# A state space mixer whose gate takes two GpSimd operations, whose squares go to ScalarE, and whose norm sums share a PSUM bank with another group's spread

## The chip, the cores and the metric

The kernel runs on one core of a Trainium2 chip, as one program and one launch. The metric is device time in microseconds (us), the median of the runs of one kernel. The engines are named as the profile names them: PE is TensorE, with PEld its weight loads, DVE is VectorE, ACT is ScalarE, POOL is GpSimd (Pool below), and SP is the engine that issues most of the DMAs.

## The reference

The trunk has two layers over a sequence of 256 tokens with a model width of 1024: `x += 1/2 SwiGLU(norm x)`, `x += mixer(norm x)`, `x += 1/2 SwiGLU(norm x)`. The mixer of layer 0 is a Mamba-2 state space mixer, that of layer 1 is latent attention. Only the first is touched by the change. Cut to what matters:

```python
proj = h @ w_in                       # 1024 -> z (2048), x and B and C (4096), dt (32)
xbc = silu(conv(xbc, conv_w, conv_b)) # depthwise, 4 taps
dt = softplus(dt + dt_bias); a = -exp(a_log)
y = ssd_chunked(xs, dt, a, bm, cm) + d_skip * xs
g = (y * silu(z)).reshape(b, s, 8, 256)
g = g * rsqrt(mean(g * g, axis=-1) + EPS)   # one norm for each of 8 groups
x = x + (g.reshape(b, s, 2048) * norm_w) @ w_out
```

The 2048 channels form 8 groups of 256 channels (4 heads of 64). Each group has a B and a C of 128 states, and a norm of its own at the end.

## The kernel before

**Data.** Channels lie on the 128 partitions, so a group of 256 channels is two halves of 128, and tokens lie along the free axis (`T` is 256). Every weight is streamed from memory once. A unit is up to eight tiles of 128x128: SP issues its DMA (`raw`), ScalarE casts it to the fast float format (`whi`, L131), and VectorE subtracts to get what the cast lost (`wlo`, L134). A product is three matmuls, high by high, high by low and low by high (`mm3`, L227 to L229), or two wider ones (L238) in the feed-forward parts. So ScalarE and VectorE owe TensorE one `whi` and one `wlo` for each unit, and everything else that they do stands in the same queues.

**The mixer.** `ssm()` has stages, called for groups 0 to 7 in an interleaved order:

- `stage_bc`, `stage_x`, `stage_z` project with the input weights. VectorE scales the projection (`up`, L421, or `zt`, L683). For B, C and x a convolution follows: ScalarE makes the first two taps (`ca` and `cb`), Pool adds them (L436), VectorE adds the other two taps (L439) and ScalarE applies Silu (L443). For z, ScalarE applies Silu alone (`zs`, L685).
- `sums` makes running sums of the decay. VectorE copies them as `bias` (L530), ScalarE as `ac` (L536), and a DMA takes them to memory (`acd`). `stage_a` fetches them for its group (`acb`, a DMA), ScalarE takes the exponentials into `dec` (L569 and L572, eight a group), and VectorE multiplies them with a product of B and C (`cbm`), L576. `stage_a` runs for two groups at a time, so there are 16 exponentials together, with a table load ahead and one behind.
- `stage_t` transposes x (`xd`, L595). `stage_y` is the scan: eight matmuls (L609 and L612), `y` on VectorE (L619), and then on Pool the gate `gt = y * zs` (L624, 128x512), two squares of 128x256 (`add_square`, L263 and L266) and their sum `gsq` (L267).
- `stage_n` sums `gsq` over the partitions on TensorE (L273, a product with ones), VectorE makes mean plus EPS (`rsv`, L277), and Pool raises it to -1/2 (`rsc`, L281).
- `stage_o` spreads `rsc` over the partitions with two transposes (L288), VectorE forms the normed `gn` (L639), and ScalarE and VectorE cut it in `yh` (L252) and `yl` (L253). `stage_out` multiplies them with the output weights into four banks that stay open through all groups.

PSUM has two pools here, each of four banks: `acc`, and `misc`, from which each call of `misc_ps()` takes the next bank. `zt`, `y` and `gn` share three buffers (tag `tmp`).

**The order.** The program is written group by group as below; a scheduler then merges the stages, so instructions of several groups alternate on each engine. Each engine runs its own queue in order, and waits on semaphores. ScalarE's functions that need a table are kept in their written order (`in_turn`).

Of the kernel before, what the change touches and what calls it, by code (L numbers as in the profile page):

```python
# [185 lines left out]
def trunk(ctx: ExitStack, tc: tile.TileContext, xt, pos, wts, small, consts, out):  # L186
# [36 lines left out]
    def misc_ps():  # L223
        return psm.tile([P, 2 * T], F32, tag="misc", name="misc")
# [41 lines left out]
        nc.gpsimd.tensor_tensor(out=sq, in0=src, in1=src, op=ALU.mult)  # L266
        nc.gpsimd.tensor_tensor(out=acc, in0=acc, in1=sq, op=ALU.add)  # L267

    def rs_col(acc, n):

        ps = misc_ps()
        for b in range(NB):
            nc.tensor.matmul(  # L273
                ps[:, b : b + 1], acc[:, b * P : (b + 1) * P], ones, start=True, stop=True
            )
        v = sp.tile([P, NB], F32, tag="rsv", name="rsv")
        nc.vector.tensor_scalar(  # L277
            out=v, in0=ps[:, :NB], scalar1=1.0 / n, scalar2=EPS, op0=ALU.mult, op1=ALU.add
        )
        r = sp.tile([P, NB], F32, tag="rsc", name="rsc", bufs=4)  # L280
        nc.gpsimd.tensor_tensor(out=r, in0=v, in1=mhalf[:, :NB], op=ALU.pow)  # L281
        return r

    def spread(r):

        ps = misc_ps()
        for b in range(NB):
            nc.tensor.transpose(  # L288
                ps[:, b * P : (b + 1) * P], r[:, b : b + 1].broadcast_to([P, P]), ident
            )  # L290
        return ps
# [113 lines left out]
    def ssm(n, nxt):  # L405
        with tc.tile_pool(name="mp", bufs=2) as mp:
# [10 lines left out]
            def conv(ps, tiles, dst):  # L417

                up = ups[count[0] % 2]
                count[0] += 1  # L420
                nc.vector.tensor_tensor(  # L421
                    out=up[:, :, KC - 1 :], in0=wide(ps), in1=pair(rs), op=ALU.mult
                )
                a = mp.tile([P, 2, T], F32, tag="ca", name="ca")
                b = mp.tile([P, 2, T], F32, tag="cb", name="cb")

                def w(t, k):
                    return sm[:, S_CW + t * KC + k : S_CW + t * KC + k + 1]

                for j, t in enumerate(tiles):  # L430
                    nc.scalar.activation(
                        a[:, j], up[:, j, 0:T], AF.Identity,
                        bias=sm[:, S_CB + t : S_CB + t + 1], scale=w(t, 0),
                    )
                    nc.scalar.activation(b[:, j], up[:, j, 1 : 1 + T], AF.Copy, scale=w(t, 1))
                nc.gpsimd.tensor_tensor(out=a, in0=a, in1=b, op=ALU.add)  # L436
                for k in (2, 3):
                    for j, t in enumerate(tiles):
                        nc.vector.scalar_tensor_tensor(  # L439
                            out=a[:, j], in0=up[:, j, k : k + T], scalar=w(t, k), in1=a[:, j],  # L440
                            op0=ALU.mult, op1=ALU.add,
                        )
                in_turn(nc.scalar.activation(dst, a, AF.Silu))  # L443
# [159 lines left out]
            def stage_y(g):  # L603
# [17 lines left out]
                        in1=ps[:, j * T : (j + 1) * T], op0=ALU.mult, op1=ALU.add,  # L621
                    )
                gt = mp.tile([P, 2, T], F32, tag="gt", name="gt")
                nc.gpsimd.tensor_tensor(out=gt, in0=y, in1=zs, op=ALU.mult)  # L624
                sq = sp.tile([P, T], F32, tag="xsq", name="gsq")
                for j in range(2):
                    add_square(sq, gt[:, j], j == 0)
                st[g, "g"], st[g, "q"] = gt, sq

            def stage_n(g):  # L630
                st[g, "r"] = rs_col(st.pop((g, "q")), 2 * P)

            def stage_o(g):
                gt = st.pop((g, "g"))
                ps = spread(st.pop((g, "r")))
                gn = mp.tile([P, 2, T], F32, tag="tmp", name="gn", bufs=3)
                for j in range(2):
                    t = 2 * g + j
                    nc.vector.scalar_tensor_tensor(  # L639
                        out=gn[:, j], in0=gt[:, j], scalar=sm[:, S_SN + t : S_SN + t + 1],  # L640
                        in1=ps[:, :T], op0=ALU.mult, op1=ALU.mult,
                    )
                yh = mp.tile([P, 2, T], F32R, tag="yh", name="yh", bufs=3)
                yl = mp.tile([P, 2, T], F32R, tag="yl", name="yl", bufs=3)
                two_part(yh, yl, gn)
                st[g, "y"] = yh, yl
# [31 lines left out]
            def stage_z(g):  # L678
# [6 lines left out]
                in_turn(nc.scalar.activation(zs, zt, AF.Silu))  # L685
                st[g, "z"] = zs

            stage_bc(1)
            last = NG - 1
            for g in range(NG):  # L690
                stage_x(g)
                if g == 0:
                    bias, acd = sums()
                if g > 1:
                    stage_o(g - 2)
                stage_z(g)
                if g:
                    stage_y(g - 1)
                if g % 2 == 0:
                    stage_a(g)  # L700
                    stage_a(g + 1)
                if g + 2 < NG:
                    stage_bc(g + 2)
                if g:
                    stage_n(g - 1)
                if g < last:
                    stage_t(g)
                if g > 2:
                    stage_out(g - 3)
# [582 lines left out]
```

## Time and profile before

| | |
|---|---|
| median of three runs | 1103.98 us (1102.43 to 1105.25) |
| the profiled execution | 1104.49 us, of which the span from first to last instruction is 1102.7 us |
| TensorE busy | 1079.8 us, 98% of the span |
| VectorE, ScalarE, Pool busy | 838.8, 643.1 and 195.7 us |
| mean granted TensorE clock | 0.992 of full speed |

The mixer with its norm runs from about 205 to 440 us of the span. The 1.8 us between the profiled execution and its span are not in the trace. A granted clock of 1.00 is TensorE's upper level, 2.4 GHz; a stretch that shows less has spent a part of itself at the lower one, 1.2 GHz.

### The profile page before, as it was taken

To read this page: it belongs to the slowest core of one execution; us is meant where nothing else is said; L and a number is where in the kernel's file an instruction comes from. 1 tells how busy PE (TensorE), PEld (TensorE's weight loads), DVE (VectorE), ACT (ScalarE), POOL (GpSimd) and SP (SyncE) were. 2 spreads that over 40 slices of the span, in tenths; PEclk is the share of its full clock that TensorE was granted. 3 is DMA by queue.
4 is the path that set the end of the run, shared out by engine and by line. 5 is a ranking of instruction groups with operands and counts; after the bars stand their busy time and mean duration, and the time that the engine had idled before them with its cause. 6 is when DMAs were issued, how large, how long until landed. Compare 5 with 4: busy or idle time off the path is not lost.

```text
span 1102.7 us, 18308 instructions
## 1 busy us (share of the span) xinstructions
PE 1079.8 (98%) x6886; PEld 964.3 (87%) x6886; DVE 838.8 (76%) x1396; ACT 643.1 (58%) x1105; POOL 195.7 (18%) x201
## 2 busy tenths in 40 slices
PE   8999999999899998999999999999999999999998
PEld 7888888998899998888888988888898688888887
DVE  7877766789978867877777688876779868877663
ACT  6755644667876744666544476664458546655541
POOL 1100013213523235000012101001240544000000
PEclk9999999999999998999999999999999999999999
DMA  8656655565445453655555566655531325656661
GB/s 287 213 189 190 184 188 170 173 197 190 161 163 178 135 185 97 208 187 184 184 191 189 174 210 211 212 196 187 175 105 59 97 87 167 214 186 188 191 200 49
DMA packets 55640, 191.58 MB, mean 174 GB/s; under 512 B 6240, under 2 KB 9088, under 8 KB 55552
## 3 DMA queue, kind: packets, MB, share of 16 engines
q1 hardware_dynamic: 55488, 190.41, 53.0%
q8 instruction: 54, 0.88, 0.3%
q14 instruction: 34, 0.28, 0.1%
q0 software_dynamic: 64, 0.01, 0.0%
HBM read 189.31 MB, written 1.08 MB: 173 GB/s over the span
## 4 chain that ended last, share of the span: by engine, by line
PE 61%; DVE 2%; ACT 0%; issue 0%; ACTq 0%; DVEq 0%
PE acc L238 32%; PE misc L238 17%; PE acc L227 2%; PE acc L228 2%; PE acc L229 2%; PE acc L1072 1%; PE acc L248 1%; PE acc L247 1%; PE acc L249 1%; PE misc L963 1%; PE misc L1032 1%; PE misc L1057 0%; DVE pr L1050 0%; DVE mx L1041 0%; PE misc L1033 0%; PE misc L273 0%
## 5 line engine op out<-in xcount | busy, mean ns | idle before, releaser
L134 DVE TENSOR_TENSOR wlo<-raw,whi 128x1024 fp32r<-128x1024 f32 (+2 forms) x345 | 429.4, 1247 | 155.0 <-ACT whi L131 153.8
L131 ACT CAST whi<-raw 128x1024 fp32r<-128x1024 f32 (+2 forms) x353 | 362.8, 1032 | 252.5 <-PE acc L238 132.9
L238 PE MATMUL misc<-xp,whi 128*128 128x512 f32 x704 | 277.9, 398 | 0.5 <-DVE xp L257 0.5
L238 PE MATMUL acc<-xp,whi 128*128 128x512 f32 x704 | 275.5, 395 | 0.0
L238 PE MATMUL acc<-ap,whi 128*128 128x512 f32 x616 | 215.5, 397 | 0.0
L238 PE MATMUL acc<-xp,wlo 128*128 128x256 f32 x704 | 196.8, 281 | 0.0
L238 PE MATMUL misc<-xp,wlo 128*128 128x256 f32 x704 | 196.4, 281 | 0.3 <-DVE wlo L134 0.2
L238 PE MATMUL acc<-ap,wlo 128*128 128x256 f32 x616 | 167.8, 281 | 0.0
L238 PEld LDWEIGHTS acc<-xp,whi 128*128 128x128 f32 x704 | 131.9, 188 | 32.2
L238 PEld LDWEIGHTS misc<-xp,whi 128*128 128x128 f32 x704 | 131.9, 188 | 24.2 <-DVE xp L257 0.8
L238 PEld LDWEIGHTS misc<-xp,wlo 128*128 128x128 f32 x704 | 132.5, 188 | 8.2 <-DVE wlo L134 0.9
L238 PEld LDWEIGHTS acc<-ap,whi 128*128 128x128 f32 x616 | 113.9, 188 | 25.5
L238 PEld LDWEIGHTS acc<-xp,wlo 128*128 128x128 f32 x704 | 132.8, 189 | 0.7
L238 PEld LDWEIGHTS acc<-ap,wlo 128*128 128x128 f32 x616 | 115.4, 188 | 2.8
L346 ACT COPY g<-misc 128x256 f32<-128x256 f32 x88 | 32.7, 371 | 77.1 <-PE misc L238 77.1
L228 PE MATMUL acc<-xp,whi 128*128 128x256 f32 x264 | 74.6, 283 | 0.0
L227 PE MATMUL acc<-xp,whi 128*128 128x256 f32 x264 | 74.5, 283 | 0.0
L229 PE MATMUL acc<-xp,wlo 128*128 128x256 f32 x264 | 74.2, 281 | 0.0
L263 POOL TENSOR_TENSOR xsq<-x 128x256 f32<-128x256 f32 x5 | 3.1, 612 | 284.8 <-DVE x L402 271.4
L266 POOL TENSOR_TENSOR sq<-x 128x256 f32<-128x256 f32 x35 | 31.7, 912 | 111.2 <-DVE x L402 111.2
L347 DVE TENSOR_TENSOR g<-misc,g 128x256 f32<-128x256 f32 x88 | 37.0, 420 | 18.0 <-ACT g L346 18.0
L227 PEld LDWEIGHTS acc<-xp,whi 128*128 128x128 f32 x264 | 49.7, 189 | 0.3 <-issue 0.3
(260 smaller groups left out, 1889.5 us busy)
## 6 DMA issues: line engine op xcount, KB each, us to landing
raw<-wts SPq DMA_DIRECT2D x341, 512.0 KB, 3.7
acb<-acd SPq DMA_DIRECT2D x8, 512.0 KB, 3.8
raw<-wts SPq DMA_DIRECT2D x8, 256.0 KB, 4.9
raw<-wts SPq DMA_DIRECT2D x4, 384.0 KB, 3.2
x<-xt SPq DMA_DIRECT2D x8, 128.0 KB, 4.5
out<-x SPq DMA_DIRECT2D x8, 128.0 KB, 3.5
raw<-wts SPq DMA_DIRECT2D x4, 192.0 KB, 2.4
sm<-small SPq DMA_DIRECT2D x1, 283.5 KB, 6.4
```

The costliest lines, as they stand in the source:

```text
L131: self.nc.scalar.copy(hi[:, c], raw[:, c])
L134: ins = eng.tensor_tensor(out=lo[:, c], in0=raw[:, c], in1=hi[:, c].bitcast(F32), op=ALU.subtract)
L227: nc.tensor.matmul(o, w[0], h, start=start, stop=False)
L228: nc.tensor.matmul(o, w[0], l, start=False, stop=False)
L229: nc.tensor.matmul(o, w[1], h, start=False, stop=stop)
L238: nc.tensor.matmul(dst, a, b, start=start and i == 0, stop=stop and i == 1)
L247: nc.tensor.matmul(o, h, w[0], start=start, stop=False)
L248: nc.tensor.matmul(o, l, w[0], start=False, stop=False)
L249: nc.tensor.matmul(o, h, w[1], start=False, stop=stop)
L266: nc.gpsimd.tensor_tensor(out=sq, in0=src, in1=src, op=ALU.mult)
L346: nc.scalar.copy(t, ps[:, T:])
L347: nc.vector.tensor_tensor(out=t, in0=ps[:, :T], in1=t, op=ALU.add)
```

## The change

The gate is written by two Pool operations of 128x256 where it was one of 128x512. The squares move from Pool to ScalarE, as one Square of 128x512 into a new tile, and Pool adds its two halves. That tile is a fourth user of the three `tmp` buffers. In the mixer's eight norms, the mean plus EPS (`rsv`) moves from VectorE to ScalarE. Pool's add in the convolution is cut in two halves as well. And the spread of group g-2, which stood ahead of `stage_z(g)`, now stands behind `stage_bc(g+2)`, next to the sums of group g-1, and both use one bank: the spread its left half, the sums its right half.

```diff
-    def rs_col(acc, n):
+    def rs_col(acc, n, ps=None, by_act=False):
-        ps = misc_ps()
+        ps = misc_ps() if ps is None else ps
...
-        nc.vector.tensor_scalar(
-            out=v, in0=ps[:, :NB], scalar1=1.0 / n, scalar2=EPS, op0=ALU.mult, op1=ALU.add
-        )
+        if by_act:
+            nc.scalar.activation(v, ps[:, :NB], AF.Copy, scale=1.0 / n, bias=EPS)
+        else:
+            nc.vector.tensor_scalar(
+                out=v, in0=ps[:, :NB], scalar1=1.0 / n, scalar2=EPS, op0=ALU.mult, op1=ALU.add
+            )
...
-                nc.gpsimd.tensor_tensor(out=a, in0=a, in1=b, op=ALU.add)
+                for j in range(2):
+                    nc.gpsimd.tensor_tensor(out=a[:, j], in0=a[:, j], in1=b[:, j], op=ALU.add)
...
-                nc.gpsimd.tensor_tensor(out=gt, in0=y, in1=zs, op=ALU.mult)
-                sq = sp.tile([P, T], F32, tag="xsq", name="gsq")
+                sq = mp.tile([P, 2, T], F32, tag="tmp", name="sq2", bufs=3)
                 for j in range(2):
-                    add_square(sq, gt[:, j], j == 0)
-                st[g, "g"], st[g, "q"] = gt, sq
+                    nc.gpsimd.tensor_tensor(
+                        out=gt[:, j], in0=y[:, j], in1=zs[:, j], op=ALU.mult
+                    )
+                nc.scalar.activation(sq, gt, AF.Square)
+                nc.gpsimd.tensor_tensor(out=sq[:, 0], in0=sq[:, 0], in1=sq[:, 1], op=ALU.add)
+                st[g, "g"], st[g, "q"] = gt, sq[:, 0]
...
+            def stage_on(g):
+                ps = misc_ps()
+                if g > 1:
+                    stage_o(g - 2, ps)
+                if g:
+                    stage_n(g - 1, ps[:, T:])
...
-                if g > 1:
-                    stage_o(g - 2)
                 stage_z(g)
...
-                if g:
-                    stage_n(g - 1)
+                stage_on(g)
```

The scheduler's result differs in more places than the diff. Three are shown. Lines of the changed kernel are a few higher: L288 is L291, L421 is L424, L439 is L443, L443 is L447, L569 and L572 are L573 and L576, L639 is L646.

TensorE at the end of the mixer, before. L273 are the sums of the last group, L288 is its spread, the rows around them multiply group 6 and then (from `x4` on) group 7 with the output weights:

```order
L227 MATMUL acc<-yh,whi 128x256
L228 MATMUL acc<-yl,whi 128x256
L229 MATMUL acc<-yh,wlo 128x256
L273 MATMUL misc<-ones,gsq 128x1 x2
L288 MATMUL misc<-cst,rsc 128x128 x2
L227 MATMUL acc<-yh,whi 128x256 x4
L228 MATMUL acc<-yl,whi 128x256
```

and the same place of the changed kernel (the spread is L291):

```order
L228 MATMUL acc<-yl,whi 128x256
L273 MATMUL misc<-ones,sq_4689 128x1 x2
L229 MATMUL acc<-yh,wlo 128x256
L227 MATMUL acc<-yh,whi 128x256
L228 MATMUL acc<-yl,whi 128x256
L229 MATMUL acc<-yh,wlo 128x256
L227 MATMUL acc<-yh,whi 128x256
L228 MATMUL acc<-yl,whi 128x256
L229 MATMUL acc<-yh,wlo 128x256
L291 MATMUL misc<-cst,rsc 128x128 x2
L227 MATMUL acc<-yh,whi 128x256 x4
L228 MATMUL acc<-yl,whi 128x256
```

The sums moved ahead of seven output matmuls of group 6, so that these seven now stand between the sums and the spread, which had stood back to back. The first product with group 7 still follows the spread directly. A little earlier, group 6's own spread and the eight scan matmuls of group 7 were followed at once by the first product with group 6; in the changed kernel twenty output matmuls of group 5 stand between.

VectorE in the first groups, before. `up_2047` is the scaled x projection of group 0, `bias` a copy of the decay's running sums:

```order
L515 SCALAR_TENSOR_TENSOR dt<-dtp,dtv 128x64
L519 SCALAR_TENSOR_TENSOR dta<-dt,am 128x64
L134 TENSOR_TENSOR wlo<-raw,whi 128x1024
L439 SCALAR_TENSOR_TENSOR ca<-up_2048,sm,ca 128x256 x2
L421 TENSOR_TENSOR up_2047<-acc,rs 128x2x256
L439 SCALAR_TENSOR_TENSOR ca<-up_2048,sm,ca 128x256
L134 TENSOR_TENSOR wlo<-raw,whi 128x1024
L439 SCALAR_TENSOR_TENSOR ca<-up_2048,sm,ca 128x256
```

and in the changed kernel:

```order
L443 SCALAR_TENSOR_TENSOR ca<-up_2048,sm,ca 128x256
L519 SCALAR_TENSOR_TENSOR dt<-dtp,dtv 128x64
L443 SCALAR_TENSOR_TENSOR ca<-up_2048,sm,ca 128x256
L523 SCALAR_TENSOR_TENSOR dta<-dt,am 128x64
L443 SCALAR_TENSOR_TENSOR ca<-up_2048,sm,ca 128x256
L134 TENSOR_TENSOR wlo<-raw,whi 128x1024
L443 SCALAR_TENSOR_TENSOR ca<-up_2048,sm,ca 128x256
L424 TENSOR_TENSOR up_2047<-acc,rs 128x2x256
L134 TENSOR_TENSOR wlo<-raw,whi 128x1024
```

`up_2047` now stands behind a `wlo` and all four taps of the convolution ahead of it, where it stood behind two of them (a `wlo` had stood ahead of those). ScalarE's `ac` copy, from which the DMA of the decay sums starts, stands behind the four ScalarE operations that read this `up`, in both kernels.

ScalarE around the exponentials of the second pair of groups, before. `dec` are the exponentials, `cbm` the product of B and C:

```order
L569 ACTIVATE dec<-acb,bias 128x256
L572 ACTIVATE dec<-acm,bias 128x128
L131 CAST whi<-raw 128x1024
L443 ACT_TABLE_LOAD
L443 ACTIVATE bc<-ca 128x512
```

and in the changed kernel, with the new Square (L633), which is that of group 1:

```order
L573 ACTIVATE dec<-acb,bias 128x256
L576 ACTIVATE dec<-acm,bias 128x128
L556 COPY cbm<-misc 128x384 x2
L131 CAST whi<-raw 128x1024
L633 ACTIVATE sq_2958<-gt 128x512
L434 ACTIVATE ca<-up_2048,sm 128x256
L438 ACTIVATE cb<-up_2048,sm 128x256
```

The Square stands behind the last of the 16 exponentials, two copies of `cbm` and a cast. Before, ScalarE had no part in that group's squares.

## Rows read from the trace of the kernel before

**Rows 1.** The page of before, part 1: busy time of each engine.
```profile
PE 1079.8 (98%) x6886; PEld 964.3 (87%) x6886; DVE 838.8 (76%) x1396; ACT 643.1 (58%) x1105; POOL 195.7 (18%) x201
```

**Rows 2.** What TensorE waited for, 255 to 440 us: total, times, longest.
```profile
PE misc L273 <- POOL gsq L267: 4.8, 4, 3.3
PE misc L288 <- POOL rsc L281: 3.2, 2, 2.2
PE acc L227 <- ACT yh L252: 2.1, 2, 1.9
PE acc L228 <- DVE yl L253: 1.1, 1, 1.1
```

**Rows 3.** Five stretches: length, busy time by engine, granted clock, DMA share, GB/s.
```profile
core 0: us, PE busy (x) PEld busy (x) DVE busy (x) ACT busy (x) POOL busy (x), PEclk, DMA share, GB/s
255.00:303.00 48.00, 42.36 (x342) 40.20 (x341) 47.55 (x63) 36.23 (x63) 24.67 (x18) 0.96 0.50 167
267.00:276.00 9.00, 6.85 (x44) 5.59 (x43) 9.00 (x17) 5.91 (x10) 1.45 (x2) 0.81 0.70 225
297.00:309.00 12.00, 8.72 (x61) 8.52 (x60) 9.37 (x13) 5.24 (x9) 6.59 (x6) 0.86 0.57 179
408.00:411.00 3.00, 1.69 (x15) 1.20 (x13) 2.77 (x5) 0.68 (x2) 0.69 (x1) 1.00 0.28 82
414.00:426.00 12.00, 9.02 (x54) 8.70 (x53) 5.79 (x9) 3.40 (x6) 2.15 (x3) 0.72 0.27 89
```

**Rows 4.** VectorE by line, 255 to 303 us: busy, mean ns, idle before.
```profile
L134 DVE TENSOR_TENSOR wlo<-raw,whi 128x1024 fp32r<-128x1024 f32 x14 | 19.8, 1425 | 0.4 <-ACT whi L131 0.4
L439 DVE SCALAR_TENSOR_TENSOR ca<-up,sm,ca 128x256 f32<-128x256 f32 x16 | 10.4, 701 | 0.0
```

**Rows 5.** VectorE by line, 309 to 345 us, where Pool has little work.
```profile
L134 DVE TENSOR_TENSOR wlo<-raw,whi 128x1024 fp32r<-128x1024 f32 x10 | 12.1, 1214 | 0.9 <-ACT whi L131 0.9
...
L439 DVE SCALAR_TENSOR_TENSOR ca<-up,sm,ca 128x256 f32<-128x256 f32 x8 | 3.5, 473 | 0.0
```

**Rows 6.** Pool's timeline: start, us, instruction, idle before and releaser.
```profile
255.70 1.30 POOL L624 TENSOR_TENSOR gt<-y,zs 128x512 f32<-128x512 f32 x1 [17.68 <-DVE y L619]
...
294.50 3.96 POOL L624 TENSOR_TENSOR gt<-y,zs 128x512 f32<-128x512 f32 x1 [3.00 <-DVE y L619]
...
412.56 0.61 POOL L266 TENSOR_TENSOR sq<-gt 128x256 f32<-128x256 f32 x1
```

**Rows 7.** VectorE's timeline: same columns.
```profile
244.14 0.69 DVE L560 TENSOR_TENSOR acb<-acb,cst 128x512 f32<-128x512 f32 x1 [2.08 <-DMA acb<-acd]
...
269.85 0.15 DVE L277 TENSOR_SCALAR rsv<-misc 128x2 f32<-128x2 f32 x1
...
341.67 0.86 DVE L639 SCALAR_TENSOR_TENSOR gn<-gt,sm,misc 128x256 f32<-128x256 f32 x2
```

**Rows 8.** ScalarE's timeline: same columns.
```profile
276.02 0.63 ACT L685 ACTIVATE zs<-zt 128x512 f32<-128x512 f32 x1
...
283.59 0.39 ACT L572 ACTIVATE dec<-acm,bias 128x128 f32<-128x128 f32 x1
```

**Rows 9.** TensorE's timeline: same columns.
```profile
249.44 0.66 PE L609 MATMUL misc<-dec,xd 128*64 128x256 f32 x4 [0.16 <-DVE dec L576]
...
262.02 0.61 PE L273 MATMUL misc<-ones,gsq 128*128 128x1 f32 x4 [0.21 <-POOL gsq L267]
...
282.48 0.50 PE L273 MATMUL misc<-ones,gsq 128*128 128x1 f32 x4
...
338.36 0.38 PE L288 MATMUL misc<-cst,rsc 128*128 128x128 f32 x2
...
416.20 0.50 PE L273 MATMUL misc<-ones,gsq 128*128 128x1 f32 x4
...
417.73 0.43 PE L288 MATMUL misc<-cst,rsc 128*128 128x128 f32 x2 [1.03 <-POOL rsc L281]
...
420.11 1.22 PE L227 MATMUL acc<-yh,whi 128*128 128x256 f32 x4 [1.95 <-ACT yh L252]
```

More of the change, by code (lines that the diff above doesn't have):

```diff
@@ L282, in rs_col, with spread @@
         return r
-    def spread(r):
-        ps = misc_ps()
+    def spread(r, ps=None):
+        ps = misc_ps() if ps is None else ps
         for b in range(NB):
@@ L623, in stage_y, with stage_n, stage_o @@
                 gt = mp.tile([P, 2, T], F32, tag="gt", name="gt")
-                nc.gpsimd.tensor_tensor(out=gt, in0=y, in1=zs, op=ALU.mult)
-                sq = sp.tile([P, T], F32, tag="xsq", name="gsq")
+                sq = mp.tile([P, 2, T], F32, tag="tmp", name="sq2", bufs=3)
                 for j in range(2):
-                    add_square(sq, gt[:, j], j == 0)
-                st[g, "g"], st[g, "q"] = gt, sq
-            def stage_n(g):
-                st[g, "r"] = rs_col(st.pop((g, "q")), 2 * P)
-            def stage_o(g):
+                    nc.gpsimd.tensor_tensor(
[4 more added lines that the diff above has]
+                st[g, "g"], st[g, "q"] = gt, sq[:, 0]
+            def stage_n(g, ps=None):
+                st[g, "r"] = rs_col(st.pop((g, "q")), 2 * P, ps, True)
+            def stage_o(g, ps=None):
                 gt = st.pop((g, "g"))
-                ps = spread(st.pop((g, "r")))
+                ps = spread(st.pop((g, "r")), ps)
                 gn = mp.tile([P, 2, T], F32, tag="tmp", name="gn", bufs=3)
```

## The prediction

> **What bounds the kernel.** First the page's busy times [rows 1]: the reader is to see TensorE at 98% and VectorE at 76%, so a change pays only where it removes TensorE's idle time or raises its clock. In the mixer behind its first scan, TensorE's waits add up to 4.8 + 3.2 + 2.1 + 1.1 = 11.2 us [rows 2]; the norm's sums wait for Pool's squares, the spread for Pool's power, the output products for the halves of `gn`. These are the chain that the change touches. Then the table of stretches [rows 3], of which three show a granted clock below 1.00: a stretch's length times what is missing is 9 x 0.19 = 1.7, 12 x 0.14 = 1.7 and 12 x 0.28 = 3.4 us, together 6.8 us. So about 18 us lie in reach.
>
> They fall into four places. Early, up to 303 us: 0.2 and 2.2 (the longest power wait) and 3.3 (the longest squares wait), plus 1.7 + 1.7 of clock. In the middle, two further squares waits, 4.8 - 3.3 - 0.2 = 1.3 us. At 408 to 411, the small rest of the wait for `yh` (2.1 - 1.9 = 0.2) and the wait for `yl` of 1.1, at full clock. At the end, 1.03 before the last spread and 1.95 before group 7's products [rows 9], with 3.4 of clock.
>
> One thing must be seen before any of that is counted as gain: from 255 to 303 us VectorE is busy 47.55 of 48 us [rows 3]. There TensorE's waits are the shadow of VectorE's list. A Pool step that gets quicker doesn't shorten that list by itself.
>
> **Prices.** A Pool operation of 128x256 alone takes 0.61 us and one of 128x512 1.30 [rows 6], so cutting the gate or the convolution's add costs nothing on Pool, and lets the reader of a half start up to 0.6 us earlier. Two squares of 0.61, which is 1.2 us a group, leave Pool. The trace has no Square of 128x512 on ScalarE; the nearest row is `zs`, 128x512, 0.63 [rows 8], which I take. `rsv` on ScalarE lies between its own 0.15 on VectorE [rows 7] and that 0.63; a 128x2 operation is nearest the small end, and I take 0.25. Eight of both are 7.0 us of ScalarE, which has idle time enough (36.23 of 48 busy in the fullest stretch [rows 3]); they cost through what queues behind them, below. The `tmp` tile adds no wait in the order that I see: `y` takes the buffer of the group before's squares, which TensorE's sums read ahead of that scan. If that cover went, `y` would wait for those sums.
>
> **Term 1, up to 303 us: -0.5.** VectorE's list is longer than its work, because Pool runs beside it: `wlo` means 1425 ns here against 1214 where Pool is quiet, the taps 701 against 473 [rows 4, 5]. That is 14 x 0.211 + 16 x 0.228 = 6.6 us. Pool's undisturbed work here is 4 adds and 3 gates of 1.30, 9 operations of 0.61, about 15 us; 6 x 0.61 = 3.7 of it goes. In proportion the list gets 6.6 x 3.7 / 15 = 1.6 shorter, and three `rsv` of 0.15 make it 2.1. Against it, two costs. (i) In group 0 the decay chain starts late: `up_2047` now stands behind two more taps, 2 x 0.47, and ScalarE's copy for the decay's DMA behind that. VectorE already waits 2.08 us for that DMA's result [rows 7], and nothing hides what it lengthens: +0.8, and the first scan, which waits 0.16 for `dec` [rows 9], is late by as much or more. (ii) Group 1's Square stands behind the 16 exponentials. By the rows of before, the last one ends at 284.0 [rows 8]; two copies, a cast of about 1, the Square and Pool's add make it 286.5, against sums at 282.5 [rows 9], which TensorE's order puts about 0.75 later: 3.3 late. But `zt`, ahead of all this, has been moved up past a `wlo`, an `up` and a `gn`, about 2.5 us; +0.8 stays. Sum -2.1 + 0.8 + 0.8 = -0.5. The 5.6 us of early waits and their clock I expect to come back under other names (`wlo`, `xd`, `dec`). Bounds: all of Pool's 3.7 us come back and neither cost bites, -3.7; the Square's 3.3 us stay whole and the decay is 1.5 late, with 2 off the list, +3.0.
>
> A rule speaks about the size. The Trainium skill, "SBUF — State Buffer", section "Who interferes with whom", says that a VectorE instruction with two SBUF inputs and a Pool instruction that reads SBUF shut each other out for a whole instruction. The trace agrees that both stretch (`wlo` above; a gate of 3.96 against 1.30 [rows 6]). By that rule each us taken from Pool is a us given back, and the term would be -2.6 rather than -0.5; by the proportion of the rows it is -0.5. That the stretch is 6.6 us where Pool has 15 speaks for the rows.
>
> **Term 2, the middle: -0.8.** The chain from `y` to the sums loses two Pool squares and one Pool add's wait for them, and gains one ScalarE step: about 1.30 + 3 x 0.61 = 3.1 becomes 2 x 0.61 + 0.63 + 0.61 = 2.5 undisturbed, and more where VectorE stretched it. The 1.3 us of waits go. New is the shared bank: TensorE's sums now wait until VectorE has read the spread beside them. Before, the spread of one middle group began at 338.36 and its `gn` ended at 342.53 [rows 9, 7], 4.2 us; in the new order group 4's sums stand some 3.7 us behind such a spread. I take 0.5 for it, between nothing (the other groups have 5 us and more) and 1.3.
>
> The Trainium skill, "PSUM — Partial Sum Buffer", section "PSUM bank collisions raise a hardware error", says why that wait can't be left out: engines must be kept from one bank at the same time, even in different columns. The trace of before, with a bank for each, has no such wait; by the rule the term is -0.8, without it -1.3.
>
> **Term 3, 408 to 411 us: -1.3.** Twenty output matmuls, each about 42.36/342 = 0.12 us [rows 3], now stand between group 6's spread with the scan and its first product, 2.4 us for a chain that was 1.3 late. Bounds -1.3 and 0.
>
> **Term 4, the end: -0.6.** From the sums to the last spread it took 417.73 - 416.20 = 1.53 us [rows 9], of which 1.03 was idle; seven matmuls (0.84) now fill it, `rsv` is 0.1 slower, so about 0.3 stays. From the spread to group 7's first product, `gn` and `yh` run as before, less the `wlo` in their way: 1.95 becomes about 1.7. `yl` came without a wait because the four products before it took 1.22 us [rows 9] at the lower clock; at the upper they are faster, and 0.4 appears. 2.98 becomes 2.4. Bounds -1.2 and +0.6.
>
> **Term 5, clock at the end: -1.7.** The two levels are 1.2 and 2.4 GHz. Idle of 2.2 us within 267 to 276 went with 1.7 us of lost clock, and 1.3 at 408 with none [rows 2, 3]. A rest of 2.4 may keep the fall or lose it; I take half of 3.4. Bounds -3.4 and 0.
>
> Sum -0.5 - 0.8 - 1.3 - 0.6 - 1.7 = **-4.9 us**: 1104.49 becomes 1099.6 for a profiled execution, and since that lay 0.5 above the median of 1103.98, **1099.1** for the median.
>
> **Rivals.**
> *The gain is eaten.* VectorE's full list sets the pace to 303 us and beyond, so the early term is +1, and the end keeps its clock loss. Then +1.0 - 0.8 - 1.3 - 0.6 + 0 = -1.7, 1102.3. For it: 47.55 of 48. Against it: from 303 us on VectorE has idle time, and the waits there go.
> *More comes back.* Term 1 reaches -2.6 and the end's clock is whole: -2.6 - 0.8 - 1.3 - 0.6 - 3.4 = -8.7, 1095.3. For it: the stretched rows [rows 4]. Against it: the decay's later start.
> *Slower.* ScalarE's queue becomes the bound in group 1. The Square comes 3.3 us late, TensorE waits that long at the sums and falls to its lower clock, as it did beside the early wait of 3.3 (1.7 lost): 5.0. Behind the Square in ScalarE's queue stand four conv taps, `yh` and the next casts, so TensorE's weights come as late once more, 5.0 again. With -2.1 from VectorE's list, -2.7 from terms 2 to 4 and -1.7 from term 5 that is +3.5: 1107.5. It decides from 6.5 us of new loss on, which the others then no longer cover. Against it: `zt` was moved up by 2.5.
>
> **Numbers.** Forecast 0.45 (its own range 1097 to 1100.7), eaten 0.30, more 0.15, slower 0.10. Three tenths of a per cent, about what a measurement here can tell from no change, are 3.3 us: faster means below 1100.7. That is 0.43 of the forecast's 0.45 and the 0.15; the rest of the forecast and the eaten gain are "same", 0.32. From the low end of "more" to the high end of "eaten", 1094.5 to 1104.0, the range leaves out the slower case and a little below: 8 in 10.
>
> **What would show it.** Right: the waits of sums for Pool in the middle gone; no wait for `yl` near 408; about 2.4 us of waiting before group 7's products; 255 to 303 us not shorter by more than 2, with waits for `dec`, `wlo` or `xd`. Wrong: sums that wait over 2 us for the Square of group 1 or for `gn`; a clock below 0.9 in a stretch that had 1.00; an early stretch shorter by 4 us, which would say that Pool, not VectorE's list, set it.

## The result and the profile after

The changed kernel takes **1095.96 us** (median of 4 runs, 1094.84 to 1096.31) against 1104.62 us (4 runs, 1102.43 to 1105.92) for the kernel before: a ratio of 0.9922, 95% interval 0.9903 to 0.9940, or 8.7 us less. Forecast were 1099.1 and a range of 1094.5 to 1104.0. The profiled execution took 1096.19 us, with a span of 1094.4.

The page's busy times after the change:

```profile
PE 1073.7 (98%) x6886; PEld 960.4 (88%) x6886; DVE 837.6 (77%) x1388; ACT 647.3 (59%) x1121; POOL 192.2 (18%) x209
```

The reader is to see that TensorE's share is as before [rows 1], but that its busy time fell by 6.1 us without one matmul less, while its idle time (span less busy) went from 22.9 to 20.7. In the second profile of each kernel it is the other way round: busy time fell from 1077.4 to 1074.0, idle time from 25.0 to 20.6. So idle time that went and matmuls that ran at the upper clock both carry the gain, and a single pair of profiles does not tell which of them is the larger part.

TensorE's waits up to the first scan, and then from 255 to 440 us (total, times, longest), which answer to [rows 2]:

```profile
PE misc L613 <- DVE dec L580: 1.4, 1, 1.4
```

```profile
PE acc L229 <- DVE wlo L134: 2.0, 1, 2.0
PE misc L273 <- POOL sq L634: 2.0, 2, 1.4
PE acc L227 <- ACT yh L252: 1.7, 1, 1.7
PE acc L227 <- DVE up L424: 1.0, 1, 1.0
PE misc L594 <- ACT xs L447: 0.5, 1, 0.5
PE acc L228 <- DVE yl L253: 0.3, 1, 0.3
```

The waits for Pool's squares fell from 4.8 to 2.0, those for `rsc` (3.2) are gone, that for `yl` is 0.3. In their place stand waits for `dec`, `wlo`, `up` and `xs`, and the sum of the second list is 7.5 where it was 11.2. The longer of the two waits for squares, 1.4, is that of group 0, whose sums waited 0.21 before [rows 9].

The five stretches of [rows 3], in the same columns (length, PE, PEld, DVE, ACT, POOL, granted clock, DMA share, GB/s):

```profile
255.00:303.00 48.00, 42.96 (x344) 41.02 (x343) 43.47 (x57) 35.18 (x64) 19.87 (x20) 0.96 0.46 153
267.00:276.00 9.00, 9.00 (x76) 8.35 (x76) 7.11 (x12) 5.89 (x14) 1.44 (x2) 1.00 0.53 179
297.00:309.00 12.00, 10.52 (x89) 10.23 (x87) 12.00 (x17) 9.47 (x16) 5.58 (x5) 1.00 0.62 202
408.00:411.00 3.00, 3.00 (x29) 3.00 (x27) 1.15 (x2) 1.05 (x1) 0.71 (x1) 1.00 0.47 172
414.00:426.00 12.00, 11.40 (x72) 10.70 (x73) 8.42 (x12) 5.32 (x11) 6.73 (x8) 0.86 0.26 89
```

The clock is 1.00 in both early stretches that had 0.81 and 0.86, and 0.86 instead of 0.72 at the end. But between the two early stretches stands a new fall, behind a wait of 2.0 for `wlo`, so that the whole stretch from 255 to 303 shows 0.96 as before. First the kernel before, then the changed one:

```profile
290.00:296.00 6.00, 6.00 (x53) 6.00 (x52) 6.00 (x11) 4.01 (x5) 3.00 (x2) 1.00 0.63 210
```

```profile
290.00:296.00 6.00, 4.43 (x25) 4.43 (x25) 6.00 (x9) 1.61 (x2) 0.43 (x1) 0.72 0.57 162
```

VectorE, which was busy 47.55 of the 48 us from 255 on, is busy 43.47. The lines of VectorE in that stretch [rows 4] show where its idle time is (line, count, busy us, mean ns, then idle before it and for whom):

```profile
L134 DVE TENSOR_TENSOR wlo<-raw,whi 128x1024 fp32r<-128x1024 f32 x13 | 17.5, 1362 | 0.0
...
L443 DVE SCALAR_TENSOR_TENSOR ca<-up,sm,ca 128x256 f32<-128x256 f32 x16 | 9.5, 617 | 0.0
...
L564 DVE TENSOR_TENSOR acb<-acb,cst 128x512 f32<-128x512 f32 x3 | 2.6, 864 | 4.5 <-ACT cbm L556 4.5
```

One gap of 4.5 us, ahead of `acb`. The taps are shorter (617 against 701 ns), `wlo` a little (1362 against 1425).

The end of the mixer, which answers to the last rows of [rows 9]:

```profile
412.15 0.43 PE L291 MATMUL misc<-cst,rsc 128*128 128x128 f32 x2
...
414.25 0.74 PE L227 MATMUL acc<-yh,whi 128*128 128x256 f32 x4 [1.67 <-ACT yh L252]
415.34 0.58 PE L228 MATMUL acc<-yl,whi 128*128 128x256 f32 x1 [0.35 <-DVE yl L253]
```

The spread no longer waits, the first product waits 1.67 instead of 1.95, and `yl` 0.35.

**Where the 8 us lie.** TensorE's sums of a norm's squares (L273 on `xsq`) mark the same places in both programs: the mixer's norm, the norm behind the mixer, the first of the attention's latents, the last norm. From the first start of each group to the next, in us, for all profiled executions of this study (the count of matmuls between a group's scan and its sums is that of the kernels' TensorE order, and the traces give the same to within two; the last column is TensorE's wait for the squares of the eight groups):

| kernel | median | mixer | attention | matmuls from scan to sums, groups 0 to 7 | wait for squares |
|---|---|---|---|---|---|
| before | 1104.6 | 240.3, again 241.3 | 115.8, 115.9 | 87 63 77 70 87 54 78 50 | 4.8, 5.9 |
| changed | 1096.0, again 1096.3 | 235.3, 234.6 | 113.9, 114.6 | 79 89 100 121 84 88 56 63 | 2.0, 1.8 |
| e1 order and bank only | 1106.8 | 242.6 | 115.8 | 87 55 100 107 84 68 77 50 | 0.6 |
| e2 squares only | 1110.0 | 245.2 | 113.8 | 82 97 50 95 77 54 68 53 | 9.3 |
| e3 all but order and bank | 1112.4 | 249.1 | 114.8 | 79 101 39 89 77 54 67 47 | 13.3 |
| d1 as e3, sums later | 1103.6 | 240.3 | 115.2 | 72 97 72 89 76 58 67 47 | 5.3 |
| e5 two banks | 1105.4 | 243.9 | 115.5 | 79 89 57 88 67 56 52 62 | 5.0 |
| e7 rsv on VectorE | 1098.3 | 235.8 | 115.2 | 79 89 100 121 84 88 56 60 | 1.8 |
| e8 squares on Pool | 1103.1 | 240.0 | 115.8 | 94 55 95 121 84 61 69 57 | 3.1 |
| f1 extra matmuls at the end | 1096.6 | 234.0 | 115.3 | as changed | 2.1 |
| h2 sums later still | 1096.9 | 235.1 | 115.8 | 72 116 136 126 104 88 56 63 | 0.5 |
| h1 combined | 1091.5 | 229.1 | 115.2 | 86 100 131 126 104 88 56 60 | 0.9 |

The stretch between mixer and attention is 366.6 in nearly all of them (365.3 to 366.9), and that behind the last norm's sums 179.6 or 179.7. Of the 8.05 us between the two mean spans (1102.55 and 1094.5), 6.45 had come in by the sums behind the mixer, and 1.6 came in the attention, which the change does not touch. Of the 6.45, 0.6 lies ahead of the mixer's first sums, which start at 200.3 and 198.9 in the two profiles of the kernel before and at 198.9 and 199.1 in those of the changed one; the mixer itself gave 5.85.

What these 5.85 are made of can be read for every kernel alike. In the mixer's stretch TensorE sat idle (length less its busy time) for 11.5 and 13.7 us before and for 9.0 and 8.2 after (the first profile of each kernel follows, before and then changed, columns as above):

```profile
200.30:440.60 240.30, 228.85 (x1838) 220.12 (x1837) 198.91 (x279) 158.98 (x260) 82.64 (x72) 0.97 0.49 163
```

```profile
198.90:434.20 235.30, 226.26 (x1838) 217.79 (x1837) 195.68 (x271) 164.56 (x278) 77.86 (x80) 0.99 0.49 166
```

The lower clock, counted as in the prediction, cost 6.8 and 5.1 before and 3.4 in both profiles after. What is left of the length is 222 to 223 us in all four profiles. It is the same in e1, e3 and e5 (idle 14.1, 19.9 and 13.0; clock 6.7, 6.9 and 8.4). So the mixer's time is TensorE's work at its upper clock, the same in each, plus its idle time, plus what the lower clock costs.

### The profile page after: what moved, and what is told of

Its sections match the earlier page's. It is cut to its first block, busy times and chain, and to the rows that moved or that the text cites. A ratio compares the mean times of both kernels' runs of the same rounds, so it can differ in the third digit from the quotient of the medians.

```text
span 1094.4 us, 18329 instructions
## 1 busy us (share of the span) xinstructions
PE 1073.7 (98%) x6886; PEld 960.4 (88%) x6886; DVE 837.6 (77%) x1388; ACT 647.3 (59%) x1121; POOL 192.2 (18%) x209
## 4 chain that ended last, share of the span: by engine, by line
PE 88%; DVE 5%; ACT 3%; DMA 2%; issue 2%; POOL 1%; SPq 0%; DVEq 0%; ACTq 0%; POOLq 0%
PE acc L238 42%; PE misc L238 22%; PE acc L227 4%; PE acc L228 4%; PE acc L229 4%; PE misc L228 2%; PE misc L227 2%; PE misc L229 2%; DVE wlo L134 1%; DVE ca L443 1%; DMA acb<-acd 1%; PE acc L1084 1%; DMA raw<-wts 1%; PE acc L248 1%; PE acc L247 1%
## 5 line engine op out<-in xcount | busy, mean ns | idle before, releaser
L238 PEld LDWEIGHTS acc<-ap,whi 128*128 128x128 f32 x616 | 113.9, 188 | 25.6
L238 PEld LDWEIGHTS acc<-xp,wlo 128*128 128x128 f32 x704 | 132.7, 188 | 0.7
L229 PEld LDWEIGHTS acc<-xp,wlo 128*128 128x128 f32 x264 | 50.5, 191 | 2.2 <-DVE wlo L134 2.2
```

The costliest lines, as they stand in the source:

```text
L229: nc.tensor.matmul(o, w[1], h, start=False, stop=stop)
L238: nc.tensor.matmul(dst, a, b, start=start and i == 0, stop=stop and i == 1)
```

## The experiments

**e1, e2, e3: the parts by themselves.** e1 puts only the order and the shared bank on the kernel before (the last part of the diff); e2 only the gate, the Square and the add:

```diff
-                nc.gpsimd.tensor_tensor(out=gt, in0=y, in1=zs, op=ALU.mult)
...
-                    add_square(sq, gt[:, j], j == 0)
+                    nc.gpsimd.tensor_tensor(out=gt[:, j], in0=y[:, j], in1=zs[:, j], op=ALU.mult)
+                nc.scalar.activation(sq, gt, AF.Square)
+                nc.gpsimd.tensor_tensor(out=sq[:, 0], in0=sq[:, 0], in1=sq[:, 1], op=ALU.add)
```

and e3 takes the order and the shared bank out of the changed kernel again:

```diff
+                if g > 1:
+                    stage_o(g - 2)
                 stage_z(g)
...
-                stage_on(g)
+                if g:
+                    stage_n(g - 1)
```

> Only the new place of the spread and the shared bank, on the kernel before: squares stay on Pool, rsv on VectorE, the convolution's add whole. Theory A (the time is TensorE's work at its upper clock, plus its idle time, plus about 1.7 us for each fall of the clock, and each part of the change removes the idle spots that hang on it): the waits for Pool's squares stay, with the fall beside the longest one, and the waits at 408 to 411 and part of those at the end go: about 2 to 3 us below before, 1101 to 1103. Theory B (the new order alone did it): 1096 to 1098. Theory C (Pool's squares off VectorE's port did it all): no change, 1104 to 1105.

> Only the gate in two Pool operations and the Square on ScalarE, on the kernel before; rsv, convolution, order and banks as before. A: the long squares wait with its fall of the clock (3.3 + 1.7) and the two in the middle (1.3) go, part of it comes back as waits for wlo; the end stays: 3 to 5 us below before, 1100 to 1102. B: no change. C: all of it, 1096 to 1097.

> The changed kernel with the spread back at its old place and a bank for each. A: the waits for yh and yl near 408 (1.3) and 0.6 at the end come back, and the end's second fall of the clock (1.7): 1099 to 1100. B: back to before, 1104. C: unchanged, 1096.

Against the kernel before, e1 gave a ratio of 1.0013 (1.0001 to 1.0024), e2 1.0047 (1.0034 to 1.0060), e3 1.0067 (1.0054 to 1.0079). All three miss what every theory expected. The two halves of the change are e1 and e3: neither gains anything alone, e1 is slower by an amount that its interval hardly tells from none, e3 clearly, and only both together gain. What fell of theory A is that each part removes its own idle spots and that these add up.

What each half lacks is in its waits. e1, waits of TensorE in the mixer (total, times, longest):

```profile
PE acc L227 <- DVE up L424: 4.9, 1, 4.9
PE acc L227 <- ACT yh L252: 2.1, 2, 1.9
PE misc L612 <- DVE xd L598: 2.1, 1, 2.1
PE misc L593 <- ACT xs L446: 2.0, 1, 2.0
PE acc L228 <- DVE yl L253: 1.1, 1, 1.1
PE misc L291 <- POOL rsc L284: 1.0, 1, 1.0
PE misc L273 <- POOL gsq L267: 0.6, 1, 0.6
```

The sums hardly wait any more. Instead TensorE waits for `up` and `xd`, which VectorE makes, and for `xs`, which ScalarE makes from VectorE's taps, and the clock falls beside the longest of these waits. The waits for `yh`, `yl` and `rsc` at the end of the mixer are those of the kernel before. e2 has the opposite: two of its sums, of groups 2 and 5, which stand 50 and 54 matmuls behind their scan (table), wait long for their squares:

```profile
303.98 0.61 PE L273 MATMUL misc<-ones,sq 128*128 128x1 f32 x4 [3.70 <-POOL sq L630]
...
384.94 1.01 PE L273 MATMUL misc<-ones,sq 128*128 128x1 f32 x4 [3.47 <-POOL sq L630]
```

And e3, at group 2, with 39 matmuls between scan and sums, the longest wait of the study:

```profile
311.09 1.02 PE L273 MATMUL misc<-ones,sq 128*128 128x1 f32 x4 [7.16 <-POOL sq L634]
```

Pool's timeline of e3 ahead of that shows why the gate itself is late:

```profile
304.75 2.06 POOL L440 TENSOR_TENSOR ca<-ca,cb 128x256 f32<-128x256 f32 x1 [12.65 <-ACT cb L438]
306.78 0.72 POOL L630 TENSOR_TENSOR gt<-y,zs 128x256 f32<-128x256 f32 x1
307.46 0.90 POOL L440 TENSOR_TENSOR ca<-ca,cb 128x256 f32<-128x256 f32 x1
308.32 0.72 POOL L630 TENSOR_TENSOR gt<-y,zs 128x256 f32<-128x256 f32 x1
```

The gate's halves alternate with the halves of a convolution's add, which had waited 12.65 us for ScalarE; the Square comes behind the second half of the gate, and Pool's sum behind the Square. In e2's group 2 the gate stands behind such an add as well (it starts at 299.88, and the scan had ended near 294). At group 5 it is ScalarE's queue that is late, as will be seen under e5.

**e7: rsv back on VectorE.**

```diff
-                st[g, "r"] = rs_col(st.pop((g, "q")), 2 * P, ps, True)
+                st[g, "r"] = rs_col(st.pop((g, "q")), 2 * P, ps)
```

> The changed kernel with rsv back on VectorE; the order of the rest is nearly the same. A: rsv stands behind VectorE's list only in the first groups, and the spread of the changed order leaves it time: 0 to 1 us slower, 1096 to 1097. A rival for the early gain (rsv on ScalarE removed the 2.2 us wait of the first spread and its fall of the clock): 1099 to 1100, with a wait of L291 for rsc near 268.

1098.26 us, ratio 0.9939 (0.9927 to 0.9951): over the 1096 to 1097 expected, and under the rival's 1099. The mixer takes 235.8 and has no wait for `rsc`, against 235.3 and 234.6: the move of `rsv` is worth 0.5 to 1.2 us at most there. The rest of the 2.3 us lies in the attention (115.2). One wait is new, at the sums of group 2:

```profile
PE misc L273 <- DVE gn L646: 0.7, 1, 0.7
```

This is the shared bank's price that term 2 reckoned with, though at another group. The changed kernel's own two profiles have no such wait.

**e5 and e8: one part taken out of the changed kernel.** e5 keeps the new place and gives sums and spread a bank each; e8 makes the squares on Pool as before.

```diff
             def stage_on(g):
-                ps = misc_ps()
                 if g > 1:
-                    stage_o(g - 2, ps)
+                    stage_o(g - 2)
                 if g:
-                    stage_n(g - 1, ps[:, T:])
+                    stage_n(g - 1)
```

> The changed kernel with the spread's new place, but a bank of its own for the sums and one for the spread. Theory D (after the first four runs: what counts is that the shared bank holds the sums back behind the spread ahead, so that a late Square is covered by other matmuls; without that, sums stand early and wait): waits of L273 for the squares of 3 us and more come back, 1099 to 1104. Theory A' (the new place of the spread is what counts, the bank only costs its wait for gn): as the changed kernel or up to 0.7 faster, 1095 to 1096.

> The changed kernel with the gate in one and the squares and their sum in three Pool operations again; rsv on ScalarE, new order, shared bank, convolution's add in halves stay. D and A' (the order makes the gain, and where the squares are made matters little once sums stand late): 1096 to 1099. Theory C' (squares on Pool hold VectorE up by the shared port, and that is most of the gain): 1101 to 1105, with wlo and the taps as long as before in the early stretch.

e5: 1105.36, ratio 1.0007 (0.9997 to 1.0017): the whole gain is gone. That is theory D's direction, but more than its 1099 to 1104, and no wait for the squares reaches the 3 us that it expected. The bank is no mere saving; in program terms it says that sums come behind the spread beside them, and the scheduler places them accordingly: 57, 88, 67, 56 and 52 matmuls behind the scan at groups 2 to 6 become 100, 121, 84, 88 and 56. TensorE's wait for the squares in e5:

```profile
PE misc L273 <- POOL sq L634: 5.0, 3, 2.8
```

The longest of them, at group 5, shows the distance at work, since the Square is equally late in both kernels. It stands in ScalarE's queue behind the 16 exponentials of the next pair of groups, and starts 8.6 us behind the last matmuls of the scan (L616). In e5, with 56 matmuls between scan and sums, TensorE waits for it:

```profile
372.58 0.44 PE L616 MATMUL misc<-dec,xd 128*64 128x128 f32 x4
...
381.19 0.62 ACT L633 ACTIVATE sq<-gt 128x512 f32<-128x512 f32 x1
...
383.29 0.60 PE L273 MATMUL misc<-ones,sq 128*128 128x1 f32 x4 [2.82 <-POOL sq L634]
```

In the changed kernel 88 stand between, and it does not:

```profile
369.54 0.44 PE L616 MATMUL misc<-dec,xd 128*64 128x128 f32 x4
...
378.16 0.62 ACT L633 ACTIVATE sq<-gt 128x512 f32<-128x512 f32 x1
...
381.02 0.50 PE L273 MATMUL misc<-ones,sq 128*128 128x1 f32 x4
```

The squares are only a part of e5's loss in the mixer, which took 8.6 and 9.3 us more than in the two profiles of the changed kernel. TensorE's idle time is 13.0 us against 9.0 and 8.2, and the clock is below 1.00 in four places (0.86, 0.72, 0.86 and 0.86 over the 12 us from 258, 300, 380 and 418) where the changed kernel has two.

e8: 1103.11, ratio 0.9987 (0.9979 to 0.9996). The shared bank is still there, and most of the gain is gone all the same; so D and A', which held that it matters little where the squares are made, missed. The time is within the expectation of C', but its sign is only half there: in the stretch from 255 to 303 us the taps take 696 ns, as long as before, while `wlo` takes 1277, less than in the changed kernel. Three waits over 2 us come back.

```profile
PE misc L291 <- POOL rsc L284: 3.5, 2, 2.5
PE misc L273 <- POOL gsq L267: 3.1, 1, 3.1
PE acc L227 <- DVE up L424: 2.8, 1, 2.8
```

The 3.1 is at group 0, although 94 matmuls stand between its scan and its sums: Pool makes the squares between the adds of a convolution and is done only at 264.7. The 2.5 is at the last spread, which follows its sums directly again, as in the kernel before. How much of e8's loss is Pool beside VectorE, and how much the other order, these runs do not separate.

**f1: no idle time for the clock to fall in.** Fourteen matmuls on `xh` (`xp` in the profile), whose results nothing reads, between the last spread and group 7's first product; group 7's products are tied behind them. The call in the program:

```diff
             stage_o(last)
             stage_out(last - 1, 6, 8)
+            fill(14)
             stage_out(last)
```

> The changed kernel with 14 extra matmuls of 128x256 between the last spread and group 7's first product, whose results nothing reads; the rest of the mixer is in the same order. The clock theory (each fall comes from the idle time just before it and costs 1.7): no clock below 1.00 at 414 to 420, and 1.5 us less than the changed kernel, 1094 to 1095. Rival (the clock falls for another reason, or the gain is no clock): 1096, with the fall in the same place.

TensorE's timeline, with the extra matmuls on L311, and two stretches (columns as above):

```profile
412.26 1.91 PE L311 MATMUL misc<-xp 128*128 128x256 f32 x14
414.17 0.74 PE L227 MATMUL acc<-yh,whi 128*128 128x256 f32 x4
```

```profile
290.00:296.00 6.00, 4.45 (x37) 4.45 (x38) 6.00 (x9) 1.77 (x2) 0.41 (x1) 1.00 0.54 160
...
412.00:420.00 8.00, 7.58 (x59) 7.17 (x60) 5.10 (x9) 4.00 (x7) 2.23 (x5) 1.00 0.42 133
```

The wait for `yh` is filled, the clock stays at its upper level, and the mixer takes 234.0, 1.3 less than the changed kernel's 235.3 and 0.6 less than its 234.6. The median, 1096.6, is no better, and over the 1094 to 1095 expected: the attention, in another order, takes 115.3. The first row of the two was not expected. At 291.55 TensorE waits 2.05 us for `wlo` as in the changed kernel, and this time the clock doesn't fall; but then it waits 2.44 instead of 1.01 for the next `up`, and reaches the sums at 302.9 instead of 303.0. So the fall there cost nothing, since VectorE, busy all of these 6 us, set the pace, and an equal wait doesn't always bring one.

**The kernels once more.**

> The kernel before once more, for a second profile. If the fall of the clock in the attention near 860 us belongs to that kernel's order, it is there again; if it is chance, not. The falls in the mixer, at 272, 302 and 418, are expected again.

> The changed kernel once more, on the chip of these runs: 1095 to 1097, 113.9 us from the latent norm's sums to the last norm's, as its order of the attention is the same. If that stretch is chance rather than order, it comes out near 115.8.

The kernel before took 1104.19 and has its fall in the attention again, a clock of 0.72 from 858 to 864 us. Its fall near 272 is not there again, the one at 300 to 308 is twice as long, and at 414 to 426 there is one fall (0.86) in place of two (0.72). The changed kernel took 1096.32 (median of 5 runs; against 15 of the kernel before the ratio is 0.9927, 0.9914 to 0.9939), and has none in the attention.

Over all profiles the attention took 113.8 to 114.6 us in the order that the scheduler gave the changed kernel and e2, and 114.8 to 115.9 in its three other orders. Which of them a kernel gets shows no relation to what was edited in the mixer. The fall is not what makes the difference: e5 and f1 have TensorE's order of the kernel before there and no fall, and took 115.5 and 115.3; h2 has a fall near 854, and took 115.8 like e1 and e8, which have its order and no fall.

**d1, h2, h1: the distance between scan and sums.** d1 is e3 with the sums called one stage later:

```diff
-                if g:
-                    stage_n(g - 1)
                 if g < last:
                     stage_t(g)
+                if g:
+                    stage_n(g - 1)
```

h2 is the changed kernel with `stage_on` one stage later:

```diff
-                stage_on(g)
                 if g < last:
                     stage_t(g)
+                stage_on(g)
```

h1 is h2 with, besides, `fill(14)`, `rsv` on ScalarE for group 0 alone, and the squares of groups 0 and 1 on Pool.

> The changed kernel with the spread at its old place and own banks, as in the third run above, but with the sums called behind the transposes of the next group: between group 2's scan and its sums TensorE has 72 matmuls in place of 39. Theory D (the distance between scan and sums decides): the wait of 7.2 us at group 2 falls below 3, the time falls by 4 to 8 us from 1112, to 1104 to 1108. Rival (the old place of the spread costs the time by itself): 1111 to 1113.

> The changed kernel with the spread and the sums one stage later still, behind the transposes: 116, 136, 126 and 104 matmuls between scan and sums of groups 1 to 4, in place of 89, 100, 121 and 84. Theory D: the mixer's stretch of 235.3 us becomes 1 to 3 shorter. The attention gets the order that took 115.8 us in two earlier runs, 1.9 more than in the changed kernel, so 1095 to 1097 in all. Rival (the distance is long enough already): 235.3 again, 1098.

> All that helped in one: sums and spread behind the transposes, squares of groups 0 and 1 on Pool (the two whose Square stands behind casts and exponentials), rsv on ScalarE for group 0 alone, 14 extra matmuls at the end whose results nothing reads. D and the clock theory: waits for squares under 0.5, no fall of the clock at the end; the mixer's stretch 231 to 233 in place of 235.3. The attention gets the order that took 114.8 and 115.2. So 1092 to 1095. Rival: VectorE's list sets the early stretch whatever is moved, 235, 1097.

d1: 1103.63, 8.8 us below e3, ratio 0.9992 (0.9978 to 1.0005). Nothing else in the source moved. Group 2's sums, which waited 7.16 us, now have no wait at all (those of groups 4 and 5 still wait 1.8 and 2.8):

```profile
302.63 0.61 PE L273 MATMUL misc<-ones,sq 128*128 128x1 f32 x4
```

h2: 1096.89, ratio 0.9930 (0.9917 to 0.9944): within its expectation in sum, but the mixer took 235.1, no less than before the edit (in a profiled execution of 1099.22, the slowest of the five). Its waits for squares fell to 0.5; a wait for `up` of 2.9 took their place. For the mixer that is the rival's result. h1: **1091.46**, ratio 0.9883 (0.9870 to 0.9897), 4.5 us below the changed kernel and the fastest of the study, 0.5 below what was expected; the mixer, too, is shorter than expected (229.1), and the waits for squares are longer (0.9). Its waits, and three stretches:

```profile
PE misc L613 <- ACT xs L466: 2.2, 2, 1.3
PE misc L632 <- DVE dec L599: 1.1, 1, 1.1
PE misc L274 <- POOL sq L663: 0.9, 1, 0.9
PE acc L228 <- DVE yl L254: 0.4, 1, 0.4
```

```profile
250.00:303.00 53.00, 49.99 (x420) 48.40 (x419) 51.18 (x71) 41.59 (x72) 28.11 (x25) 1.00 0.53 177
303.00:400.00 97.00, 97.00 (x825) 94.35 (x825) 78.91 (x111) 69.21 (x113) 28.80 (x30) 1.00 0.52 172
400.00:428.00 28.00, 27.52 (x194) 25.16 (x192) 21.62 (x25) 14.60 (x23) 18.06 (x19) 1.00 0.40 129
```

No clock below 1.00, 4.6 us of waiting in all, and VectorE busy 51.18 of 53 us early on: it is near its limit there once more. The mixer is 5.5 to 6.2 us shorter than in the changed kernel. Of h1's four parts two were tried alone: the later stage in h2 (no gain in the mixer) and the extra matmuls in f1 (0.6 to 1.3 us). The other two, Pool's squares for groups 0 and 1 and `rsv` on ScalarE for group 0 alone, were not, so most of h1's gain is not put down to a part.

## Why the prediction was right, and where its sizes were wrong

The direction and the range held. The size was 4.9 where 8.7 was measured, outside the forecast's own 1097 to 1100.7, with these terms (two profiles of each kernel; the scans of groups 3 and 6, the first product with group 7 and the norm's sums behind the mixer as marks):

- **Term 1, up to the scan of group 3** (317.3 to 315.6 on average): -1.7 where -0.5 was forecast. Of this, 0.6 lies ahead of the mixer, so the mixer's part is -1.1; from its first sums to that scan the two profiles of the kernel before alone take 117.2 and 118.2. Cost (i) came larger, a wait of 1.4 for `dec` at the first scan where 0.8 was reckoned, cost (ii) with 0.5 at group 1's sums, and a third was not in the sum: group 0's sums wait 1.4 for their Square. The waits came back under other names, as forecast (`wlo`, `dec`, and `up` and `xs`). With the wait for `wlo` came a sign that the prediction had called wrong, a clock below 0.9 in a stretch that had 1.00 (290 to 296); f1 shows that this fall cost nothing. Together the costs were larger than reckoned, and the term is lower all the same: what was mis-sized is at least the shortening of VectorE's list. Measured as the prediction sized it, `wlo` over 1214 ns and the taps over 473 from 255 to 303 us, the list's stretch is 6.6 and 6.5 us in the profiles of the kernel before and 4.2 and 3.3 in those of the changed one; 2.3 to 3.3 came back where 1.6 was forecast. By the Trainium skill's rule ("SBUF — State Buffer", section "Who interferes with whom") all 3.7 come back and the term was -2.6; the measured stretch and the measured -1.1 lie between. Pool's squares are not all of it: e8, which has them again, shows 4.4. How these sizes and the single waits add up to -1.1 is not shown.
- **Term 2, from there to the scan of group 6**: -2.2 (75.9 to 73.7) where -0.8 was forecast. The squares waits went entirely, 1.4 and in the second profile 2.2. The 0.5 for the shared bank did not appear: group 3's spread starts at 350.12, its `gn` is done at 353.42, and group 4's sums start at 354.12. e7 shows the same kind of wait with 0.7. The guard that the Trainium skill's rule on banks asks for ("PSUM — Partial Sum Buffer", section "PSUM bank collisions raise a hardware error") is thus seen in e7's trace as a wait for `gn`, and cost the changed kernel nothing.
- **Terms 3 and 4, up to the first product with group 7**: -2.5 (27.2 to 24.65) against -1.9. Term 3 was right to a tenth. In term 4 the seven matmuls hid all of the wait for `rsc`, where 0.3 was left in the forecast. The new place of the spread and the shared bank do not bring this alone: e1 has both, and keeps all of these waits.
- **Term 5, the clock at the end**: about -0.1 (20.05 to 19.95) where -1.7 was forecast. This step failed. The 3.4 us of lost clock that the prediction read at 414 to 426 are 1.7 in the second profile of before, and 1.7 remain in both profiles after: the term took for the kernel's what only one execution had.
- **Left out**: the attention, -1.6. The text of the change doesn't touch it and the prediction has no term for it, but the scheduler gave it another order.

The sum is -1.7 - 2.2 - 2.5 - 0.1 - 1.6 = -8.1, against 8.05 between the spans. Of this, 1.6 in the attention and 0.6 ahead of the mixer were luck: nothing that the prediction reasoned about brought them. Without these two the time would have been near 1098, inside the forecast's own range. Its errors cancelled in part there: in the mixer terms 1 to 4 gave 5.8 where 3.2 was forecast, and term 5 gave 0.1 where 1.7 was.

Of the rivals, "more comes back" (1095.3) was nearest, but by luck: neither of its two conditions came about, since term 1 did not reach -2.6 and the end's clock is not whole. "Slower" names a mechanism that the parts alone show, though at other groups: a Square that comes late in ScalarE's queue, with sums that wait for it, 3.5 us in e2 and 3.2 in e3 at group 5. The longest wait, 7.2 at e3's group 2, is another thing, a gate that is late on Pool. What kept the changed kernel out of both is a part that the prediction priced only as a bank's wait. The prediction took the shared bank for a cost; e5 shows that without it the gain is gone, and e1 and e8 show that the bank alone, or with the squares on Pool, does not bring it either. d1, where sums called later gave back 8.8 us without a shared bank, and group 5 in e5 and in the changed kernel speak for the distance between scan and sums as the way in which the bank works.

## What to carry to other kernels

Where a result goes through several engines before TensorE reads it, compare the time that it takes with the time of the matmuls that stand between its producer and its reader. A count alone does not tell: in the changed kernel 56 matmuls cover group 6, whose Square starts 3.8 us behind its scan, while e5's 56 at group 5, with a Square 8.6 us behind, leave a wait of 2.8, and e8's 94 at group 0 one of 3.1. A dependency that only orders things (here a shared bank) can be worth more than the work that an edit saves, where a scheduler decides what stands between. And judge parts of a change together: two halves that alone made the kernel 0.1% and 0.7% slower made it 0.8% faster together here (0.1% is at the edge of what these runs tell from none), and parts of the program that nobody edited moved by 1 to 2 us with the order that they happened to get.

## What the runs showed of the hardware

The prediction's prices for operations not seen before were right or high: Square of 128x512 on ScalarE took 0.62 to 0.63 us (0.63 taken), the small copy of 128x2 with scale and bias 0.16 to 0.17 (0.25 taken). A wait by itself does not settle whether TensorE's clock falls: the same wait of 2.05 us at 291.6 came with a fall in the changed kernel and without one in f1, and the kernel before had a fall near 272 in one of its two profiles, though the spread waits 2.15 us just ahead of it in both. A fall can also cost nothing where TensorE is not what sets the pace: the sums of group 2 start at 303.0 with the fall at 292 and at 302.9 without it, and the attention took 115.8 with a fall in h2 and without one in e1 and e8.
